# First layer's output, up and down projections: the second layer's order of products, wider products, and new places for weights and activations

## The chip, the cores and the metric

The kernel runs on one core of one Trainium2 chip. The metric is the device time of one execution in microseconds (us). Before the change it is 2280.66 us, the median of 3 runs (2280.07 to 2280.93).

## The reference

A decoder trunk of two layers over 272 positions (16 learned meta tokens and 256 inputs), width 2048, 16 heads of 128, MLP width 8192, all in float32. Cut to what matters here:

```python
a = rms_norm(h, norm_attn[0])
q, k, v, f = split(a @ fox_w_in[0])                # layer 0: forgetting attention
h = h + forgetting_attention(q, k, v, f) @ fox_w_o[0]
h = h + squared_relu(rms_norm(h, norm_mlp[0]) @ w_up[0]) @ w_down[0]
k, v = split(rms_norm(h, kv_norm) @ w_kv)          # layer 1: stick-breaking attention
q = rms_norm(h, norm_attn[1]) @ sb_w_q[0]
h = h + stick_breaking_attention(q, k, v) @ sb_w_o[0]
h = h + squared_relu(rms_norm(h, norm_mlp[1]) @ w_up[1]) @ w_down[1]
return rms_norm(h, final_norm)[:, 16:]
```

The first layer computes all 272 positions. The second layer's queries and all that follows need only the last 256, since the meta tokens are cut off at the end.

## The kernel before

Activations lie feature-major: 128 features on the partitions, 16 chunks of features, positions along the row. A product (`gemm_matmul`, line 190) is one 128x128 block of weights held in TensorE against one chunk of activations that streams past, 272 columns wide in the first layer (`t0` is 0) and in the K/V projection, 256 in the rest of the second layer (`t0` is 16). One word is 4 bytes.

**Two parts per number.** Each weight and each activation is split into a high and a low part, and three products are made: high by high, high weight by low activation, low weight by high activation. A weight block comes from HBM by a DMA on the SP queue (line 214) into `raw`; ScalarE writes the high part `whi` (line 225) and VectorE the low part `wlo` (line 226).

**A group** (`gemm_group`, line 230) makes 512 output features: 4 accumulators of PSUM (index `m`), 16 chunks of the inner dimension in 4 blocks `kb` of 4 chunks `kc`, 3 products each: 4 x 16 x 3 = 192 products. In blocks 0 and 3 the accumulators are taken one after the other, in blocks 1 and 2 all four over two chunks at a time (lines 248 to 251).

**The order of products** inside such a run differs (lines 255 to 258). In the first layer all products of one accumulator come first, and the three parts of a chunk follow one another. In the second layer the part is outermost: high by high over all chunks and accumulators of the run, then high by low, then low by high.

**The wider products** (lines 261 to 269). In the second layer, in the first group of each four (`u % 4 == 1`, where `u` numbers the groups), three products read 6 columns more, 262, from a pad of zeros that GpSimd (POOL) writes behind each chunk (line 135). The additional columns of the accumulator are not read.

**Places.** An x tile (`Split`, line 121) holds 16 chunks at a pitch of 640 words; the high part begins at `hi` and the low part at `lo`, 320 words on, from `ROWS`: (48, 368) in the first layer, (0, 320) in the second. A weight tile (line 217) has a pitch of 576 words per chunk, and its block begins at word `o1`: 0 in the first layer, 16 in the second. All x and weight buffers begin on a multiple of 64 words (256 bytes). There are two x buffers: one holds the input of a stage, the other its output.

**The stages around the change.** `out_proj` (line 612) makes the first layer's attention output, 4 groups, with input tile `o0`, and writes the tile `m0`. `mlp` (line 624) goes over the 8192 inner features in four quarters `f`: 4 groups of up projection from `m0`, whose evacuation squares and splits into the tile `u0_f` (lines 635 to 642), then 4 groups of down projection from `u0_f`, added to the residual. That makes 36 groups in the first layer's three projections. The three projections of the second layer use the same functions with `t0` = 16.

TensorE runs its instructions in program order. The order is fixed by the tile scheduler at build time, and `gemm_matmul` pins each product behind the one before it.

Of the kernel before, what the change touches and what calls it, by code (L numbers as in the profile page):

```python
# [24 lines left out]
N_FF = 4  # L25

ROWS = {0: (48, 368), M: (0, 320)}
XROW = 640

G_A0, G_M0, G_KV, G_A1, G_M1, G_FIN = range(6)  # L30
# [3 lines left out]
def yoco_kernel(ctx: ExitStack, tc: tile.TileContext, hT_in, gains, b_f, w_f, w_qkv0, w_o0, w_up, w_dn,  # L34
# [86 lines left out]
    class Split:  # L121


        def __init__(self, label, t0):
            n = T - t0
            self.t0 = t0
            rows = xs.tile([P, NC * XROW + 64], F32R, tag="x", name=f"x_{label}")
            hi, lo = ROWS[t0]
            rows = rows[:, hi:hi + NC * XROW].rearrange("p (c t) -> p c t", c=NC)
            d = lo - hi  # L130
            self.hi, self.lo = rows[:, :, :n], rows[:, :, d:d + n]
            if t0:

                self.wide = rows[:, :, :n + 6]
                nc.gpsimd.tensor_copy(rows[:, :, n:n + 6], pad[:, :6].unsqueeze(1).to_broadcast([P, NC, 6]))
# [65 lines left out]
    def weights(u, kb, wblk, o1, load_x=None):  # L201

        src_w = wblk[kb].rearrange("p (k c) -> p k c", k=4)
        piece = 1 if load_x is not None and kb < 2 else 2
        raws = [wraw.tile([P, 2, 512], F32, tag="raw", name=f"raw_{u}_{kb}_{hf}") for hf in range(2)]
        for k0 in range(0, 4, piece):
            if load_x is not None:
                load_x(range(4 * kb + k0, 4 * kb + k0 + piece))
            if load_x is not None and kb == k0 == 0:

                for c0 in (0, 256):
                    nc.scalar.dma_start(raws[0][:, 0, c0:c0 + 256], src_w[:, 0, c0:c0 + 256])
            else:
                nc.sync.dma_start(raws[k0 // 2][:, k0 % 2:k0 % 2 + piece], src_w[:, k0:k0 + piece])
        parts = []
        for hf in range(2):
            whi, wlo = (wspl.tile([P, 2, 576], F32R, tag=f"w{x}", name=f"w{x}_{u}_{kb}_{hf}") for x in ("hi", "lo"))
            whi, wlo = whi[:, :, o1:o1 + 512], wlo[:, :, o1:o1 + 512]
            boxes = [(o, piece, 0, 512) for o in range(0, 2, piece)]
            if load_x is not None and kb == hf == 0:  # L220
                boxes[:1] = [(0, 1, 0, 256), (0, 1, 256, 512)]
            for o, no, c0, c1 in boxes:
                src = raws[hf][:, o:o + no, c0:c1]
                hp, lp = whi[:, o:o + no, c0:c1], wlo[:, o:o + no, c0:c1]
                on_act = nc.scalar.activation(hp, src, AF.Copy)  # L225
                on_dve = nc.vector.tensor_tensor(out=lp, in0=src, in1=hp.bitcast(F32), op=ALU.subtract)  # L226
            parts.append((whi, wlo))
        return parts, on_act, on_dve

    def gemm_group(wblk, sp, t0, evac, before={}, after={}, load_x=None):  # L230

        uid[0] += 1
        u = uid[0]
        accs = [pacc.tile([P, 512], F32, tag="acc", name=f"acc_{u}_{m}") for m in range(4)]
        n = T - t0
        for kb in range(4):
            if kb in before:
                before[kb]()  # L240
            parts, on_act, on_dve = weights(u, kb, wblk, 16 if t0 else 0, load_x)
            if kb in after:
                with tc.issue_after(on_act.ins), tc.issue_after(on_dve.ins):
                    after[kb]()

            if load_x is not None and kb == 0:
                runs = [([kc], range(4)) for kc in range(4)]
            elif kb in (0, 3):
                runs = [(range(4), [m]) for m in range(4)]
            else:  # L250
                runs = [(range(2 * hf, 2 * hf + 2), range(4)) for hf in range(2)]
            pinned[0] = load_x is None
            for kcs, ms in runs:
                pairs = ((0, sp.hi), (0, sp.lo), (1, sp.hi))
                if t0:
                    products = [(kc, m, *pair) for pair in pairs for kc in kcs for m in ms]
                else:
                    products = [(kc, m, *pair) for m in ms for kc in kcs for pair in pairs]
                left = {m: 3 * len(kcs) for m in ms}

                wide = [(0, 0, 0), (1, 0, 1), (2, 1, 1)] if t0 and u % 4 == 1 else []
                if u == 90:

                    wide = [(0, 0, 0), (0, 0, 1), (0, 2, 1)]
                for kc, m, part, x in products:
                    first, left[m] = kb == kc == 0 and left[m] == 3 * len(kcs), left[m] - 1
                    nw = n
                    if m == (0 if u == 90 else 3) and x is sp.hi and (kb, kc, part) in wide:
                        x, nw = sp.wide, n + 6
                    gemm_matmul(accs[m][:, :nw], parts[kc // 2][part][:, kc % 2, m * P:(m + 1) * P], x[:, 4 * kb + kc],  # L270
                                start=first, stop=kb == kc == 3 and left[m] == 0)
                if kb == 3:
                    for m in ms:
                        evac(m, accs[m][:, :n])
# [39 lines left out]
    def load_x(chunks):  # L314
        c0, n = chunks[0], len(chunks)
        nc.sync.dma_start(hT[:, c0:c0 + n, :], hT_in[:, c0:c0 + n, :])
        if c0 == 0:
            nc.sync.dma_start(g_sb, gains)
        for c in chunks:
            split_chunk(xa, G_A0, c)  # L320
# [140 lines left out]
    ao = Split("o0", 0)  # L461
    for g in range(4):
# [11 lines left out]
        if g == 0:  # L474

            gemm_group(w_qkv0[0], xa, 0, lambda m, acc, qT=qT: nc.scalar.copy(qT[:, m, :], acc),
                       after={kb: (lambda kb=kb: first_norm(kb)) for kb in range(4)}, load_x=load_x)
# [12 lines left out]
        def decays(j):  # L490

            for i, (o, n) in enumerate(((0, 144), (144, T))):
# [5 lines left out]
                   after={j: (lambda j=j: decays(j)) for j in range(4)})  # L498
# [113 lines left out]
    def out_proj(w, ao, t0, gi, label):  # L612
        norm = Norm(label, t0)
        xm = Split(label, t0)
        for g in range(4):
            def evac(m, acc, g=g):
                c = 4 * g + m
                residual_add(c, acc, t0)
                split_chunk(xm, gi, c)
                norm.add(c)  # L620
            gemm_group(w[g], ao, t0, evac)
        return xm, norm

    def mlp(layer, xm, norm, t0, last_evac, last_group=None):
        box = {}

        def get_rstd():
            box["r"] = norm.finish()

        for f in range(N_FF):  # L630
            u = Split(f"u{layer}_{f}", t0)
            for g in range(4):
                def evac(m, acc, g=g):
                    c = 4 * g + m
                    r = tmp.tile([P, T], F32, tag="relu", name=f"relu_{layer}_{f}_{c}")
                    u2 = tmp.tile([P, T], F32, tag="u2", name=f"u2_{layer}_{f}_{c}")
                    nc.vector.scalar_tensor_tensor(out=r[:, t0:], in0=acc, scalar=0.0, in1=box["r"][:, t0:],
                                                   op0=ALU.max, op1=ALU.mult)
                    nc.scalar.activation(u2[:, t0:], r[:, t0:], AF.Square)
                    nc.scalar.activation(u.hi[:, c], u2[:, t0:], AF.Copy)  # L640
                    nc.vector.tensor_tensor(out=u.lo[:, c], in0=u2[:, t0:], in1=u.hi[:, c].bitcast(F32),
                                            op=ALU.subtract)
                gemm_group(w_up[layer, f, g], xm, t0, evac, {2: get_rstd} if f == g == 0 else {})
                if last_group is not None and f == N_FF - 1 and g == 0:
                    to_token_major()
            for g in range(4):
                def evac(m, acc, g=g):
                    residual_add(4 * g + m, acc, t0)
                    if f == N_FF - 1:
                        last_evac(4 * g + m)  # L650
                if last_group is not None and f == N_FF - 1 and g == 3:
                    last_group(w_dn[layer, f, g], u)
                else:
                    gemm_group(w_dn[layer, f, g], u, t0, evac)

    xm, norm_m = out_proj(w_o0, ao, 0, G_M0, "m0")


# [16 lines left out]
    for g in range(4):  # L675
# [4 lines left out]
        def split_c(kb, g=g):  # L680
            for c in ([4 * kb + g - 1] if g < 3 else [4 * kb + 2, 4 * kb + 3]):
# [3 lines left out]
                   after={kb: (lambda kb=kb: split_c(kb)) for kb in range(4)} if g else {})  # L685

    ao = Split("o1", M)
# [123 lines left out]
    xm, norm_m = out_proj(w_o1, ao, M, G_M1, "m1")  # L811
# [28 lines left out]
    def last_group(wblk, u):  # L840
        ob = xs.tile([P, NC * XROW + 64], F32, tag="x", name="ob")[:, :2 * D].rearrange("p (b d) -> p b d", b=2)

# [108 lines left out]
```

## Time and profile before

| what | value |
|---|---|
| timed runs, median of 3 | 2280.66 us |
| profiled execution, first to last instruction (span) | 2278.5 us |
| TensorE busy, share of the span | 2271.1 us, 100% |
| VectorE busy | 1333.5 us, 59% |
| ScalarE busy | 1065.1 us, 47% |
| GpSimd busy | 39.4 us, 2% |
| mean DMA rate | 187 GB/s |

The profile shows one execution. For the profiled execution the page gives the span; the time of a run is some 2 us longer than it. PE is TensorE's matmul, PEld its load of the stationary block. Matmuls overlap, so the duration of one (near 280 ns) is longer than the time from the start of one to the start of the next, and busy time says little here: the number to read is the time of a stretch divided by its count of products. The chain of work that ended last gives such stretches, as start, length, engine, tile, line and count.

### The profile page before, as it was taken

The numbers are of one execution on the slowest core, as the hardware profiler recorded it, in microseconds if no ns is written. First come the engines' busy times: TensorE is split into PE (matmuls) and PEld (weight loads), VectorE is DVE, ScalarE is ACT, GpSimd is POOL, SyncE is SP. The second block draws the span as 40 slices with busy tenths as digits, with TensorE's granted clock in tenths as the row PEclk, the third lists the DMA queues.
The fourth block names the chain that finished last, engine by engine and source line by source line (L and its number), as shares of the span: only waits on it lengthen the run. The fifth ranks groups of instructions, "written<-read, shape, count | busy, mean of one in ns | idle before, by whom it ended". The sixth has DMA issues, their size and how long they took to land.

```text
span 2278.5 us, 44956 instructions
## 1 busy us (share of the span) xinstructions
PE 2271.1 (100%) x18898; PEld 2262.8 (99%) x18898; DVE 1333.5 (59%) x1930; ACT 1065.1 (47%) x1471; POOL 39.4 (2%) x72
## 2 busy tenths in 40 slices
PE   9999999999999999999999999999999999999998
PEld 9999999999999999999999999999999999999998
DVE  7767566554455455455566666666555555555555
ACT  6444445443354344335445555555443544543554
POOL 1000000000000000000000000000000000000001
PEclk9999999999999999999999999999999999999999
DMA  7765665555555555555556555555656556566564
GB/s 238 228 198 188 222 184 176 181 172 180 182 176 185 167 185 179 174 185 169 186 183 193 168 174 169 167 185 190 202 187 201 192 189 201 184 200 195 186 201 141
DMA packets 146171, 425.19 MB, mean 187 GB/s; under 512 B 31648, under 2 KB 43824, under 8 KB 145968
## 3 DMA queue, kind: packets, MB, share of 16 engines
q1 hardware_dynamic: 113760, 406.29, 54.1%
q10 hardware_dynamic: 32208, 16.02, 2.6%
q8 instruction: 148, 2.42, 0.4%
q14 instruction: 55, 0.45, 0.1%
HBM read 413.85 MB, written 8.41 MB: 185 GB/s over the span
## 4 chain that ended last, share of the span: by engine, by line
PE 99%; DMA 0%; issue 0%; POOL 0%; SPq 0%; POOLq 0%; ACT 0%; DVE 0%
PE acc L192 97%; PE po L435 0%; PE ps L435 0%; PE pza L435 0%; DMA raw<-w_qkv 0%; PE pzb L735 0%; PE po L804 0%; PE ps L508 0%; PE po L603 0%; PE pf L354 0%; PE pta L757 0%; PE pta L756 0%; PE pv L394 0%; POOL ob L850 0%; PE ptb L709 0%
## 5 line engine op out<-in xcount | busy, mean ns | idle before, releaser
L226 DVE TENSOR_TENSOR wlo<-raw,whi 128x1024 fp32r<-128x1024 f32 (+1 forms) x773 | 928.5, 1216 | 715.6 <-ACT whi L225 706.6
L225 ACT ACTIVATE whi<-raw 128x1024 fp32r<-128x1024 f32 (+1 forms) x773 | 796.4, 1050 | 961.0 <-PE acc L192 913.4
L192 PE MATMUL acc<-x_m,whi 128*128 128x272 f32 (+1 forms) x4096 | 643.1, 282 | 0.0
L192 PE MATMUL acc<-x_u,whi 128*128 128x272 f32 (+1 forms) x3968 | 626.0, 282 | 0.0
L192 PEld LDWEIGHTS acc<-x_m,whi 128*128 128x128 f32 x4096 | 566.0, 188 | 0.1
L192 PEld LDWEIGHTS acc<-x_u,whi 128*128 128x128 f32 x3968 | 550.4, 188 | 0.0
L192 PE MATMUL acc<-x_m,wlo 128*128 128x272 f32 (+1 forms) x2048 | 441.4, 282 | 0.0
L192 PE MATMUL acc<-x_u,wlo 128*128 128x272 f32 (+1 forms) x1984 | 432.1, 282 | 0.0
L192 PE MATMUL acc<-x_a,whi 128*128 128x272 f32 (+1 forms) x2048 | 355.4, 286 | 0.2 <-ACT whi L225 0.2
L192 PEld LDWEIGHTS acc<-x_m,wlo 128*128 128x128 f32 x2048 | 323.5, 188 | 0.0
L192 PEld LDWEIGHTS acc<-x_u,wlo 128*128 128x128 f32 x1984 | 315.3, 188 | 0.0
L192 PEld LDWEIGHTS acc<-x_a,whi 128*128 128x128 f32 x2048 | 301.3, 189 | 1.7 <-ACT whi L225 1.1
L192 PE MATMUL acc<-x_a,wlo 128*128 128x272 f32 (+1 forms) x1024 | 253.8, 286 | 0.0
L192 PE MATMUL acc<-x_kv,whi 128*128 128x272 f32 x1024 | 191.7, 288 | 0.0
L192 PEld LDWEIGHTS acc<-x_a,wlo 128*128 128x128 f32 x1024 | 175.7, 188 | 0.7 <-DVE ssq_a L158 0.4
L192 PE MATMUL acc<-x_o,whi 128*128 128x272 f32 (+1 forms) x1024 | 163.1, 283 | 0.0
L192 PEld LDWEIGHTS acc<-x_kv,whi 128*128 128x128 f32 x1024 | 160.1, 189 | 0.1
L192 PE MATMUL acc<-x_kv,wlo 128*128 128x272 f32 x512 | 147.6, 288 | 0.0
L192 PEld LDWEIGHTS acc<-x_o,whi 128*128 128x128 f32 x1024 | 142.3, 188 | 0.0
L307 DVE TENSOR_TENSOR hT<-acc,hT 128x272 f32<-128x272 f32 (+1 forms) x156 | 67.3, 431 | 75.4 <-PE acc L192 75.2
L192 PE MATMUL acc<-x_o,wlo 128*128 128x272 f32 (+1 forms) x512 | 110.7, 282 | 0.0
L192 PEld LDWEIGHTS acc<-x_kv,wlo 128*128 128x128 f32 x512 | 96.6, 189 | 0.0
(255 smaller groups left out, 1065.5 us busy)
## 6 DMA issues: line engine op xcount, KB each, us to landing
raw<-w_up SPq DMA_DIRECT2D x256, 512.0 KB, 3.9
raw<-w_dn SPq DMA_DIRECT2D x256, 512.0 KB, 4.0
raw<-w_qkv SPq DMA_DIRECT2D x92, 512.0 KB, 4.3
raw<-w_o SPq DMA_DIRECT2D x64, 512.0 KB, 3.9
raw<-w_kv SPq DMA_DIRECT2D x64, 512.0 KB, 4.4
raw<-w_q SPq DMA_DIRECT2D x32, 512.0 KB, 4.7
p_dram<-raw_p ACTq DMA_DIRECT2D x32, 96.0 KB, 4.6
v_dram<-turned ACTq DMA_DIRECT2D x48, 64.0 KB, 3.8
```

The source lines that it names most:

```text
L192: ins = nc.tensor.matmul(*args, **kw).ins
L225: on_act = nc.scalar.activation(hp, src, AF.Copy)
L226: on_dve = nc.vector.tensor_tensor(out=lp, in0=src, in1=hp.bitcast(F32), op=ALU.subtract)
L307: nc.vector.tensor_tensor(out=hT[:, c, t0:], in0=acc, in1=hT[:, c, t0:], op=ALU.add)
```

## The change

The three projections of the first layer get the second layer's order of products (`series=True`) and its wider products (here 278 columns, still in the first group of each four), and the places of activations and weights are given per tile and per quarter:

| stage | hi, lo of the x tile | weight offset |
|---|---|---|
| output projection, before | 48, 368 | 0 |
| output projection, after | 0, 320 | 16 |
| up, quarters 0, 1, 2, 3, before | 48, 368 in all | 0 in all |
| up, quarters 0, 1, 2, 3, after | 0, 320 in all | 16, 0, 48, 32 |
| down, quarters 0, 1, 2, 3, before | 48, 368 in all | 0 in all |
| down, quarters 0, 1, 2, 3, after | 0, 320; 48, 368; 16, 336; 32, 352 | 16, 0, 16, 16 |

Every x tile but the first (`a0`) now gets its pad of zeros. The two x buffers change roles throughout the program. The number of products, the weights, the q/k/v, K/V and query projections, attention and the second layer's groups keep their code.

```diff
 ROWS = {0: (48, 368), M: (0, 320)}
+ROWS_OF = {"o0": (0, 320), "m0": (0, 320), "u0_0": (0, 320), "u0_2": (16, 336), "u0_3": (32, 352)}
...
-            hi, lo = ROWS[t0]
+            hi, lo = ROWS_OF.get(label, ROWS[t0])
...
-            if t0:
+            if label != "a0":
 
                 self.wide = rows[:, :, :n + 6]
                 nc.gpsimd.tensor_copy(rows[:, :, n:n + 6], pad[:, :6].unsqueeze(1).to_broadcast([P, NC, 6]))
...
-    def gemm_group(wblk, sp, t0, evac, before={}, after={}, load_x=None):
+    def gemm_group(wblk, sp, t0, evac, before={}, after={}, load_x=None, shift=None, series=None):
...
+        series = bool(t0) if series is None else series
...
-            parts, on_act, on_dve = weights(u, kb, wblk, 16 if t0 else 0, load_x)
+            parts, on_act, on_dve = weights(u, kb, wblk, shift if shift is not None else 16 if t0 else 0, load_x)
...
-                if t0:
+                if series:
                     products = [(kc, m, *pair) for pair in pairs for kc in kcs for m in ms]
...
-                wide = [(0, 0, 0), (1, 0, 1), (2, 1, 1)] if t0 and u % 4 == 1 else []
+                wide = [(0, 0, 0), (1, 0, 1), (2, 1, 1)] if series and u % 4 == 1 else []
...
-            gemm_group(w[g], ao, t0, evac)
+            gemm_group(w[g], ao, t0, evac, shift=16, series=True)
...
-                gemm_group(w_up[layer, f, g], xm, t0, evac, {2: get_rstd} if f == g == 0 else {})
+                gemm_group(w_up[layer, f, g], xm, t0, evac, {2: get_rstd} if f == g == 0 else {},
+                           shift=16 if t0 else (16, 0, 48, 32)[f], series=True)
...
-                    gemm_group(w_dn[layer, f, g], u, t0, evac)
+                    gemm_group(w_dn[layer, f, g], u, t0, evac, shift=16 if t0 else (16, 0, 16, 16)[f], series=True)
```

## The prediction

> **What bounds the kernel now.** I read the page's first part and chain first, then the waits of TensorE, then the chain in order of time, whose pieces give a time and a count of products together.
>
> ```profile
> span 2278.5 us, 44956 instructions
> ...
> PE 2271.1 (100%) x18898; PEld 2262.8 (99%) x18898; DVE 1333.5 (59%) x1930; ACT 1065.1 (47%) x1471; POOL 39.4 (2%) x72
> ...
> PEclk9999999999999999999999999999999999999999
> ...
> PE 99%; DMA 0%; issue 0%; POOL 0%; SPq 0%; POOLq 0%; ACT 0%; DVE 0%
> ```
>
> The page: TensorE is busy for the whole span, at full granted clock in every slice, and is 99% of the chain. Nothing else ends late. The waits of TensorE, all of them:
>
> ```profile
> PE idle L61 <- DVE mean_w L57: 1.1, 1, 1.1
> PE pr_fin L192 <- DVE fin L863: 0.8, 1, 0.8
> PE acc L192 <- ACT whi L225: 0.2, 1, 0.2
> ```
>
> So 2.1 us of 2278.5 are waits for data. The time is the number of products times the time from one product's start to the next; call that the step. The count does not change, so the question is what the change does to the step. The chain cut to stretches of one kind (start, us, what, count):
>
> ```profile
> 499.96 600.14 PE acc L192 x4866
> ...
> 609.97 80.05 PE acc L192 x649
> ...
> 704.94 80.17 PE acc L192 x650
> ...
> 1599.92 60.18 PE acc L192 x531
> ...
> 1493.92 2.83 PE acc L192 x24
> ...
> 1581.78 2.47 PE acc L192 x21
> ...
> 143.06 9.12 PE acc L192 x72
> ...
> 2246.88 7.33 PE acc L192 x32
> ```
>
> Row by row. Up and down of the first layer, 272 columns: 600.14/4866 = 123.33 ns. The same in an up stage (80.05/649 = 123.34) and a down stage (80.17/650 = 123.34), which read two different x buffers, so the buffer does not matter. Second layer, 256 columns, after the wider products: 60.18/531 = 113.33. Second layer before its first wider product: 2.83/24 = 117.9 and 2.47/21 = 117.6, say 117.8. A stretch of the q/k/v products of the first layer, 272 columns, the same code as its neighbours: 9.12/72 = 126.67. The last group, 512 columns: 7.33/32 = 229.1.
>
> What the reader is to see: for one width the step is not one number but one of a few, each held for dozens to thousands of products without scatter: 113.33 or 117.8 at 256 columns, 123.33 or 126.67 at 272. TensorE is in one of several states, and the question is in which the changed projections run. The mean duration of one product (last number before the last bar) tells the state too, and there are rows of it where a stretch is too short to count steps:
>
> ```profile
> L192 PE MATMUL acc<-x_m,whi 128*128 128x272 f32 x1594 | 295.1, 287 | 0.0
> ...
> L192 PE MATMUL acc<-x_a,whi 128*128 128x272 f32 x50 | 9.5, 290 | 0.0
> ...
> L435 PE MATMUL ps<-x_o,q x48: 286/289/384, 58.1 to 297.2; 128*128 128x272 f32 x48
> ...
> L435 PE MATMUL pza<-x_o,k x48: 277/280/287, 1289.3 to 1469.4; 128*128 128x256 f32 x48
> ...
> L192 PE MATMUL acc<-x_m,whi 128*128 128x256 f32 x337 | 43.4, 276 | 0.0
> ```
>
> 287 ns goes with a step of 123.33, 290 with 126.67; at 256 columns 276 goes with 113.33.
>
> **The change part by part.**
>
> Which products. Output projection 4 groups, up 16, down 16: 36 groups of 192 products, 6912 in all, each of 272 columns at 123.33 ns now, 852.5 us of the span. Everything else keeps its code; its x tiles swap buffers, which costs nothing by the rows of up and down above.
>
> Places. Let the distance be x offset less weight offset, in words modulo 64; chunk pitch 640, weight pitch 576, column block 128 and the 320 between hi and lo are multiples of 64, and all these buffers start on multiples of 256 bytes, so one distance holds for a whole group. Before, it is 48 - 0 = 48 in the first layer and 0 - 16 = 48 in the second. After: output 48; up by quarter 0-16, 0-0, 0-48, 0-32, that is 48, 0, 16, 32; down 0-16, 48-0, 16-16, 32-16, that is 48, 48, 0, 16. So 16 groups (3072 products) stay at 48 and 20 groups (3840 products) go elsewhere.
>
> The 3072 products at 48. Only the order and the wider products are new. Below they could fall to a state like the second layer's 113.33, above they could go to 126.67. By columns: the two states without lock, 117.8 at 256 and 229.1 at 512, differ by 111.3 ns over 256 columns, 0.435 ns per column; 113.33 + 16 x 0.435 = 120.3 ns would be the locked step at 272 columns, an estimate. The bounds are -3.0 and +3.3 ns, -9.3 and +10.2 us. I take 0: 123.33 holds through all 4866 products of the first row above without a push, and it lies nearer to a lock than the 117.8 + 7.0 = 124.7 that the columns give for a free run.
>
> The 3840 products elsewhere. No projection of the trace runs there. The nearest rows are attention's: its products at line 435 read the same x tiles against other stationary tiles, whose distances work out to 8 words (ps) and 24 words (pza). The 272-column one has a median of 289 where 48 has a mean of 287 and the slow stretch 290: two thirds of the way, 123.33 + 2.2 = 125.6 ns. The 256-column one has 280, against 276 locked. They are short runs between other work, so this is weak, but no row at a distance other than 48 shows a lock. Bounds: 120.3 if they lock (-11.6 us), 126.67 (+12.8 us); the free run of 124.7 gives +5.3. I take +2.2 ns: 3840 x 2.2 = +8.5 us.
>
> Order of products. The same 192 products, weights and sums. In blocks 0 and 3 the third product now needs chunk 2 of the weights where the seventh did, 4 steps or 0.5 us earlier. The waits above hold one wait of 0.2 us for a weight split in 2278 us, and the second layer runs this order at a shorter step without any, with as much split work per group (DVE and ACT have 59% and 47%). Cost 0; if that cover went, each late half would show as a wait of DVE or ACT at line 225 or 226.
>
> Wider products. The first group of each four from the output projection on has three of them: 9 x 3 = 27, each 6 columns more, 6 x 0.435 = 2.6 ns, 0.07 us, and in the state they leave there may be a settling step or two of some ns. I take 0.1 us.
>
> The pad copies that they read.
>
> ```profile
> L135 POOL CAST x_u<-pad x4: 267/267/268, 1570.5 to 2093.5; 128x96 fp32r<-128x96 f32 x4
> ...
> 1478.64 0.48 POOL L135 CAST x_m<-pad 128x96 fp32r<-128x96 f32 x1 [26.13 <-PE acc L192]
> 1479.48 1.15 POOL L446 COPY pk_vc<-vT 128x128 f32<-128x128 f32 x1 [0.36 <-DVE vT L472]
> ```
>
> Seven more copies on POOL of 0.27 to 0.48 us, each waiting for the last reader of its buffer. Behind that of x_m stand the packing copies of v, which TensorE's transposes need. The second layer has this very sequence: the copy behind it waited 0.36 us for DVE's v, not for the pad. Cost 0.
>
> Sum, on the profiled execution: 0 + 8.5 + 0.1 = +8.6 us on a span of 2278.5. The median of the timed runs is 2280.66, 2.2 us more than the span, for what lies around it; the sum goes on that: 2289.3 us.
>
> Two rules speak against any effect. The Trainium skill, SBUF — State Buffer, Who interferes with whom, says that TensorE reads moving and stationary operands through two independent ports and never waits on anyone; by that rule places change nothing and the time would be 2280.8. The Trainium skill, TensorE: Matmul & The Clock Gate, Back-to-back issue gap, gives columns/2.4 + 2.5 ns; by it 272 columns take 115.8 and the time would again not depend on places. The trace does not agree with the second (123.33 and 126.67 at one width and clock), and no run here shows the first.
>
> **The rivals.**
>
> (A) Lock everywhere. The wider product puts TensorE into a state that holds, as it does in the second layer; it decides at the first group of each four, up of quarter 0 for instance, and 768 products run at what it left. Price 6912 x -3.04 = -21.0 us: 2259.7, clearly faster. For it: the second layer goes from 117.8 to 113.33 at its wider products and keeps it through every stage. Against it: no 272-column row is below 123.33, though attention's products break and restart the q/k/v products again and again, and 123.33 may already be the 272-column form of that state.
>
> (B) Lock at distance 48 only, the others as now: 3072 x -3.04 = -9.3 us, 2271.4. With the others at +8.5, 2280.0, no change.
>
> (C) The change doesn't do what it says: neither order nor place moves the state, 2280.8.
>
> (D) The order loses 123.33 everywhere: 6912 x 3.33 = +23.0 us, 2303.8. For it: 126.67 is a stable state of the same width, held for 72 products and more in the trace, and a wider product may throw TensorE into it. Against it: in the first layer's long stages it never occurs.
>
> **How the numbers follow.** Forecast, 48 unchanged and the rest slower by 1.4 to 3.3 ns (2286 to 2294): 0.36. A 0.21, B with the others as now 0.14, B with the others slower 0.06, C 0.07, D 0.16. Against the 0.2% (4.6 us) that a measurement of this kernel can tell from no change: faster, A and B, 0.35; the same, 0.13 (C and the mixed B); slower, the forecast and D, 0.52. Cases of both signs hold much of this, so the range runs from A to a little over the forecast's upper bound, 2258 to 2297, and leaves out D; the forecast's own range is 2286 to 2294.
>
> **What would show it.** In the changed trace the chain in order of time, cut by half quarter (768 products each, now 94.7 us). Forecast: output, up 0, down 0 and down 1 at 123.3 ns; up 1, up 2, up 3, down 2 and down 3 between 124.7 and 126.7 (95.8 to 97.3 us). A shows as 92.4 us in each, C as 94.7, D as 97.3. Mean durations near 290 go with the slow state, near 284 with a lock. The forecast is wrong if a distance other than 48 runs below 123.3, if 48 leaves 123.3, or if TensorE gains waits at line 225, 226 or on POOL.

## The result, and the profile after

The changed kernel takes 2291.24 us (median of 4 runs, 2290.35 to 2291.56), the kernel before 2280.80 in the same sessions: a ratio of 1.0045, 95% interval 1.0030 to 1.0059. It is slower by 10.4 us, 0.45%. The profiled execution has a span of 2289.8 us, 11.3 more than before.

The page of the changed kernel, first parts:

```profile
span 2289.8 us, 44970 instructions
...
PE 2282.2 (100%) x18898; PEld 2273.8 (99%) x18898; DVE 1336.8 (58%) x1930; ACT 1065.5 (47%) x1471; POOL 42.4 (2%) x79
...
PEclk9999999999999999999999999999999999999999
```

TensorE is still busy throughout at full clock, with the same 18898 records. Its waits in the changed kernel:

```profile
PE idle L62 <- DVE mean_w L58: 1.1, 1, 1.1
PE pr_fin L193 <- DVE fin L866: 0.8, 1, 0.8
PE acc L193 <- ACT whi L226: 0.4, 1, 0.4
```

They come to 2.3 us against 2.1, so these waits do not make the 11.3 us (what the opening of the kernel adds stands below). The chain in order of time, one stretch from each stage (start, us, engine, tile, line, count of products); from the top: output; up and down of quarter 0; up and down of quarter 1; the same of quarters 2 and 3.

```profile
349.95 60.06 PE acc L193 x487
...
428.39 71.67 PE acc L193 x581
...
514.99 80.08 PE acc L193 x649
...
609.93 80.10 PE acc L193 x639
...
709.99 80.07 PE acc L193 x649
...
799.99 80.06 PE acc L193 x632
...
899.89 80.21 PE acc L193 x640
...
1000.00 80.05 PE acc L193 x632
...
1094.99 80.05 PE acc L193 x632
```

Divide: 123.33 ns in the output projection, 123.36 and 123.39 in up 0 and down 0, **125.35 in up 1** (distance 0), 123.37 in down 1, **126.68 in up 2** (16), **125.33 in down 2** (0), **126.66 in up 3** (32), **126.66 in down 3** (16). What the reader is to see: within the same 80 us the count falls from 649 to 639 or 632, and it does so exactly in the stages whose distance is not 48.

The whole difference, by the starts of the groups in both traces: 2 x 1.55 us at distance 0 and 3 x 2.55 at 16 and 32, 10.74 in all; the four stages at 48 together +0.23; three stretches of the v projections -0.25 each, -0.74; a delay among the q projections +0.15; and the opening of the kernel +0.94 (the second group starts at 33.58 us instead of 32.64). The last of these moves from run to run: in the experiments' profiles the second group starts between 32.23 and 33.31. It is probably most of why the profiled spans differ by 11.3 and the medians by 10.4.

### The profile page after: what moved, and what is told of

It is laid out like the page before. It is cut to its first block, busy times and chain, and to the rows that moved or that the text cites. A ratio compares the mean times of both kernels' runs of the same rounds, so it can differ in the third digit from the quotient of the medians.

```text
span 2289.8 us, 44970 instructions
## 1 busy us (share of the span) xinstructions
PE 2282.2 (100%) x18898; PEld 2273.8 (99%) x18898; DVE 1336.8 (58%) x1930; ACT 1065.5 (47%) x1471; POOL 42.4 (2%) x79
## 4 chain that ended last, share of the span: by engine, by line
PE 99%; DMA 1%; issue 0%; POOL 0%; DVE 0%; ACT 0%; POOLq 0%; SPq 0%; DVEq 0%; ACTq 0%
PE acc L193 96%; DMA raw<-w_qkv 1%; PE po L437 0%; PE ps L437 0%; PE pza L437 0%; PE pzb L738 0%; PE po L807 0%; PE ps L510 0%; PE po L605 0%; DMA hT<-hT_in 0%; PE pf L356 0%; PE pta L760 0%; PE pta L759 0%; PE pv L396 0%; POOL ob L853 0%
## 5 line engine op out<-in xcount | busy, mean ns | idle before, releaser
L193 PE MATMUL acc<-x_m,whi 128*128 128x256 f32 (+2 forms) x4096 | 552.3, 282 | 0.0
L193 PE MATMUL acc<-x_u,whi 128*128 128x272 f32 (+1 forms) x3968 | 533.5, 282 | 0.0
L193 PEld LDWEIGHTS acc<-x_m,whi 128*128 128x128 f32 x4096 | 515.7, 188 | 0.1
L193 PEld LDWEIGHTS acc<-x_u,whi 128*128 128x128 f32 x3968 | 498.4, 188 | 0.0
L193 PE MATMUL acc<-x_m,wlo 128*128 128x272 f32 (+1 forms) x2048 | 307.0, 282 | 0.0
L193 PE MATMUL acc<-x_u,wlo 128*128 128x272 f32 (+1 forms) x1984 | 297.1, 282 | 0.0
L193 PEld LDWEIGHTS acc<-x_m,wlo 128*128 128x128 f32 x2048 | 270.8, 188 | 0.0
L193 PEld LDWEIGHTS acc<-x_u,wlo 128*128 128x128 f32 x1984 | 261.8, 188 | 0.0
L639 DVE SCALAR_TENSOR_TENSOR relu<-acc,rstd_m 128x272 f32<-128x272 f32 (+1 forms) x128 | 55.5, 433 | 77.2 <-PE acc L193 76.7
L641 ACT ACTIVATE u<-relu 128x272 f32<-128x272 f32 (+1 forms) x128 | 53.9, 421 | 92.4 <-DVE relu L639 92.4
```

The costliest lines, as they stand in the source:

```text
L193: ins = nc.tensor.matmul(*args, **kw).ins
```

## The experiments

Theory **D**: the step of a 272-column product is set by the distance, x offset less weight offset modulo 64 words, and by nothing else in the change. Its rivals are named in each expectation. A wait or a delay that is put down to a place in the program is a difference between the starts of groups in that run's trace and in the trace of before. All steps below are time over count of a stretch of the chain.

**1. Order and wider products alone.**

```diff
-ROWS_OF = {"o0": (0, 320), "m0": (0, 320), "u0_0": (0, 320), "u0_2": (16, 336), "u0_3": (32, 352)}
+ROWS_OF = {}
...
-            gemm_group(w[g], ao, t0, evac, shift=16, series=True)
+            gemm_group(w[g], ao, t0, evac, series=True)
...
-                           shift=16 if t0 else (16, 0, 48, 32)[f], series=True)
+                           series=True)
```

(and the same for the down projection.)

> The changed kernel's order of products and wider products in the first layer's output, up and down projections, at the places of before (distance 48 in all 36 groups). Theory D (the step of a 272-column product is set by the distance, x offset less weight offset modulo 64 words): all 36 groups at 123.33 ns but for a few settling steps at the wider products, 94.72 us per stage of 768 products, 0.05 us more in each, the whole within 1 us of the kernel before. Rival O (the order or the wider products cost the time, the places do not): the up and down stages lengthen as in the changed kernel, by 1.5 to 2.6 us in at least five of eight, about 10 us in all.

The chain, a stretch of up 2 and one of down 3:

```profile
799.99 80.08 PE acc L193 x649
...
1084.89 80.21 PE acc L193 x650
```

The steps are 123.39 and 123.40 ns over these stretches, and 123.33 in the groups of these two stages that have no wider products. The run took 2281.74 us beside 2280.75 for the kernel before. Its profiled span is 1.5 us longer than that of before: 0.97 us of this is one wait near the start of the second head group, 0.15 the opening, and 0.35 the changed stages. The wait does not belong to the change: it is absent in the second experiment, and 1.10 us in the ninth, which leaves the first layer alone. Each up or down stage after the first lasts 94.76 us instead of 94.72; the 0.040 us are the price of three wider products. Order and wider products cost 0.35 us in all; rival O is out as the cause.

**2. Places alone.** `series=True` is taken out of the three calls, so that order and widths are those of before:

```diff
-                           shift=16 if t0 else (16, 0, 48, 32)[f], series=True)
+                           shift=16 if t0 else (16, 0, 48, 32)[f])
```

> The changed kernel's places with the order of before and no wider product in the first layer. Theory D: the steps of the changed kernel come back, 123.33 ns in up 0, down 0, down 1, 125.3 in up 1 and down 2 (distance 0), 126.67 in up 2, up 3 and down 3 (distances 16 and 32), about 10.7 us over the kernel before. Rival O: 123.33 ns in all stages and no loss.

The chain, up 1, down 1, up 2, down 2:

```profile
609.94 80.09 PE acc L193 x639
...
704.89 80.17 PE acc L193 x650
...
799.95 80.05 PE acc L193 x632
...
899.96 80.09 PE acc L193 x639
```

The steps are 125.34, 123.34, 126.66 and 125.34 ns: those of the changed kernel, without its order and its wider products. The run took 2290.82 us, 10.1 more than the kernel before. The places alone make the loss.

**3. Both moved together.**

```diff
+ROWS_OF = {"o0": (32, 352), "m0": (16, 336), "u0_0": (0, 320), "u0_1": (16, 336), "u0_2": (32, 352), "u0_3": (48, 368)}
...
+            gemm_group(w[g], ao, t0, evac, shift=16 if t0 else 48, series=True)
...
+                           shift=16 if t0 else 32, series=True)
...
+                    gemm_group(w_dn[layer, f, g], u, t0, evac, shift=16 if t0 else (16, 32, 48, 0)[f], series=True)
```

> The changed kernel with other places again, but weights and x moved together: x at words 32, 16, 0, 16, 32, 48 and weights at 48, 32, 16, 32, 48, 0, so that the distance is 48 in all 36 groups. Theory D: 123.33 ns in all stages, within 1 us of the kernel before. Rival P (the place of the weights or of x alone sets the step, for instance weights at words 0, 32 and 48 of the 64 being bad against x at 0): 125 ns or more in the stages whose weights stand at 32 or 48, up to 12 us in all.

Up 2 (weights at 32, x at 16) and down 2 (weights at 48, x at 32):

```profile
799.97 80.08 PE acc L193 x649
...
894.97 80.07 PE acc L193 x649
```

Both have 123.4 ns, and the run took 2280.73 us beside 2280.75. With weights at 32 and 48, x at 16 and 32, the loss is gone: rival P is out. Four pairs of places at distance 48 give one step here, and in the changed kernel the two pairs at distance 0 agree with each other, and so do the two at 16. For places that are multiples of 16 words it is the distance that counts in these stages, not either place.

**4. Finer distances.** Up: weights at 8, 24, 40, 56 against x at 0; down: x at 4, 60, 12, 20 against weights at 16.

```diff
+ROWS_OF = {"o0": (0, 320), "m0": (0, 320), "u0_0": (4, 324), "u0_1": (60, 380), "u0_2": (12, 332), "u0_3": (20, 340)}
...
+                           shift=16 if t0 else (8, 24, 40, 56)[f], series=True)
```

> The changed kernel with eight other distances in up and down of the first layer: up 56, 40, 24, 8, down 52, 44, 60, 4; output at 48. Theory D alone gives values between the neighbours measured at 48, 0, 16, 32 (123.33, 125.35, 126.67, 126.67 ns): 52 near 123.8, 56 near 124.3, 60 near 124.8, 4 near 125.7, 8 near 126.0, 24 at 126.67, 40 near 125, 44 near 124.2. Rival Q (only whole blocks of 16 words count): each distance runs like one of the four. Rival L (a lock exists for 272 columns at some finer distance): one stage at about 120.3 ns, 92.4 us for its 768 products.

Distances in order of time 56, 52, 40, 44, 24, 60, 8, 4:

```profile
444.97 65.11 PE acc L193 x514
...
544.91 65.11 PE acc L193 x514
...
639.98 65.12 PE acc L193 x528
...
734.99 65.12 PE acc L193 x528
...
829.92 65.17 PE acc L193 x520
...
925.00 65.12 PE acc L193 x521
...
1019.90 65.12 PE acc L193 x518
...
1114.95 65.08 PE acc L193 x523
```

The steps are 126.67, 126.67, 123.33, 123.33, 125.33, 124.99, 125.71 and 124.44 ns. This is neither a smooth curve (52 and 56 are as slow as 16) nor blocks of 16 words (40 and 32 differ), and no stage runs at 120.3: both refinements, theory D with values between its neighbours and rival Q, fell, and rival L has no support yet. The run took 2292.68 us.

**5. Eight further distances**, by the same kind of edit (up: weights 52, 44, 36, 28; down: x 54, 58, 62, 2), and then **6. eight distances again, made the other way** (up: weights 18, 22, 14, 26; down: x 44, 36, 52, 28).

> The changed kernel with eight further distances: up 12, 20, 28, 36, down 38, 42, 46, 50; output at 48. After the fine scan (40, 44, 48 at 123.33 ns, 52, 56, 16, 32 at 126.67, 0 and 24 near 125.4) the theory is that a band of distances from 40 to 48 holds 123.33 and nothing goes below: 42 and 46 at 123.33, 12 and 20 between 125.3 and 126.67, 28 and 50 at 126.67 or near it, 36 and 38 show the lower edge of the band. Rival L (a lock at a distance not yet tried): one stage at about 120.3 ns, 92.4 us for its 768 products.

Of experiment 5, distance 28 (up 2), 42 (down 1), 46 (down 2), 20 (up 1):

```profile
829.94 65.12 PE acc L193 x528
...
734.96 65.12 PE acc L193 x528
...
924.92 65.11 PE acc L193 x514
...
639.95 65.16 PE acc L193 x519
```

123.33, 123.33, 126.67 and 125.55 ns; 12 gave 125.71, and 36, 38 and 50 gave 126.67. The band from 40 to 48 is wrong, since 46 is slow and 28 is fast.

> The distances of the run with further distances, made the other way: up 46, 42, 50, 38 now by weights at words 18, 22, 14, 26 against x at 0 (there by x at 62, 58, 2, 54), down 28, 20, 36, 12 now by x at 44, 36, 52, 28 against weights at 16 (there by weights at 36, 44, 28, 52). Theory D, that the distance alone counts, also below 16 words: the same steps again, up 126.67, 123.33, 126.67, 126.67 ns, down 123.33, 125.6, 126.67, 125.7. Rival P (below 16 words the place of x or of the weights itself counts, or the history of the state does): at least two of the eight differ by more than 0.5 ns.

Of experiment 6, distance 46 (up 0), 42 (up 1), 50 (up 2), 36 (down 2) and 20 (down 1), made the other way:

```profile
444.99 65.12 PE acc L193 x528
...
634.97 65.08 PE acc L193 x523
...
824.99 65.12 PE acc L193 x528
...
919.97 65.08 PE acc L193 x523
...
729.93 65.13 PE acc L193 x521
```

123.33, 124.44, 123.33, 124.44 and 125.01 ns, where the same distances had 126.67, 123.33, 126.67, 126.67 and 125.55. Six of eight differ (12 too, 125.0 against 125.7); 28 and 38 came out the same. So theory D holds in these stages for places that are multiples of 16 words and falls below that. There what ran before counts. The trace of experiment 4 shows it within the first group of down 1 (distance 44), whose places do not change. Its wider products are the 37th, the 68th and the 120th; before the first, between the first and the last, and after the last:

```profile
706.58 4.32 PE acc L193 x35
...
711.65 9.37 PE acc L193 x74
...
721.92 8.14 PE acc L193 x66
```

That is 123.43, 126.62 and 123.33 ns at one pair of places: the step changes at one wider product and changes back at another (no run leaves them out here). So two makings of one distance can differ by what ran before them. Whether the places themselves count as well, these runs do not tell. In none of the 24 stages of the three runs is a step under 123.33; the two runs took 2295.27 and 2287.61 us.

**7. The second layer at the changed kernel's distances** (256 columns, on the kernel before).

```diff
-            hi, lo = ROWS[t0]
+            hi, lo = {"u1_1": (16, 336), "u1_2": (32, 352), "u1_3": (48, 368)}.get(label, ROWS[t0])
...
+                           shift=(16, 0, 48, 32)[f] if t0 else 0)
```

> The kernel before, with the second layer's up and down (256 columns, its order and wider products kept) at distance 48 in quarter 0, 0 in quarter 1, 16 in quarter 2 and 32 in quarter 3. Theory D: distance 48 keeps 113.33 ns (up 0, down 0); the others lose the lock and run at 117 ns or more, 2.8 us or more longer per stage of 768 products. Rival W (the wider products lock 256 columns at any distance): 113.33 ns in all.

Down 0 (distance 48), up 1 (0), up 2 (16), down 3 (32):

```profile
1684.96 55.08 PE acc L192 x486
...
1769.94 65.16 PE acc L192 x543
...
1959.99 55.12 PE acc L192 x468
...
2204.94 50.08 PE acc L192 x422
```

The steps are 113.33, 120.00, 117.78 and 118.67 ns, and the run took 2304.69 us. The other stages at these distances agree: 120.00 in down 1, 117.78 in down 2, 118.71 in up 3. The wider products do not bring 113.33 to other distances; rival W is out. Here distance 0 is the worst, at 272 columns it is the mildest of the three.

**8. Widths.** Zeros behind each chunk, and all products of the second layer's up and down widened into them; the added columns are read by nobody.

```diff
+                    if width is not None:
+                        nw = width + more
+                        x = (sp.rows_lo if x is sp.lo else sp.rows_hi)[:, :, :nw]
...
+                           width=(264, 272, 280, 260)[f] if t0 else None)
...
+                    gemm_group(w_dn[layer, f, g], u, t0, evac, width=(258, 268, 276, 288)[f] if t0 else None)
```

> The kernel before, with the second layer's up and down products widened by columns of zeros that nobody reads: up 264, 272, 280, 260 columns by quarter, down 258, 268, 276, 288; distance 48, order and pushes kept. Theory N (the 113.33 ns belongs to 256 columns, and 272 at distance 48 runs at 123.33 wherever it stands): up 1 at 123.33 ns, the others near 113.33 + 0.42 to 0.63 ns per column. Rival S (the lock belongs to the second layer's stage, and any width keeps its 6.7 ns over the columns' own time): up 1 at 120.3, the others at 113.33 + 0.43 ns per column: 114.2 at 258, 115.1 at 260, 116.8 at 264, 118.5 at 268, 122.0 at 276, 123.7 at 280, 127.1 at 288.

Widths 264, 258, 272, 268, 280 and 288:

```profile
1594.99 65.04 PE acc L197 x542
...
1689.98 60.05 PE acc L197 x497
...
1784.99 60.06 PE acc L197 x487
...
1879.89 65.23 PE acc L197 x515
...
1979.90 60.19 PE acc L197 x467
...
2239.94 70.12 PE acc L197 x526
```

The steps are 120.00, 120.83, 123.33, 126.66, 128.89 and 133.31 ns; 260 had 120.00 and 276 had 126.67. At 272 columns the second layer, with its order and wider products, runs at the first layer's 123.33: rival S is out. Two columns more than 256 cost 7.5 ns, and 268 is slower than 272. Theory N was right on 272 and wrong on the widths around it. The run took 2347.24 us.

**9. What holds the second layer's 113.33.** Quarter 1 in the first layer's order, quarter 2 without wider products, quarter 3 with both edits. The group behind the transposes (`u` = 90), which has three wider products of its own, loses them too.

```diff
-                if t0:
+                if t0 and not (73 <= u < 81 or u >= 89):
...
-                wide = [(0, 0, 0), (1, 0, 1), (2, 1, 1)] if t0 and u % 4 == 1 else []
+                wide = [(0, 0, 0), (1, 0, 1), (2, 1, 1)] if t0 and u % 4 == 1 and u < 81 else []
-                if u == 90:
+                if False:
```

> The kernel before with the second layer's quarters altered, all at distance 48: quarter 1 in the first layer's order of products, quarter 2 in its own order without wider products, quarter 3 with the first layer's order and without wider products. Theory D with a state that lasts: 113.33 ns in quarters 1 and 2, and in quarter 3 until the transposes of the token-major tail break the stream; whether 113.33 comes back after them without a wider product shows what the push is for. Rival H (the order holds the lock): 117.8 ns or more in up 1 and down 1 already, 3.4 us more per stage.

Up 1, up 2, and up 3 after the transposes:

```profile
1749.98 80.03 PE acc L192 x706
...
1924.89 80.13 PE acc L192 x707
...
2117.64 62.46 PE acc L192 x551
```

The steps are 113.36, 113.34 and 113.36 ns, and rival H is out. The run took 2281.88 us beside 2280.43; in its profile the wait near the start of the second head group is 1.10 us longer than in that of before. Neither the order nor the wider products are needed to keep the step, and after the transposes it came back by itself, within a few products. It is otherwise at three breaks earlier in the second layer, where the trace of before shows 117.8 for some 20 products (two of them are in the prediction's rows): there each such stretch ends at a wider product. Whether it would end without one was not tried.

**10. The gain inside the loss.** In the kernel before, the v projections of heads 4 to 15 each have a stretch at 126.67; in the changed kernel it is gone. One of them, in the kernel before and then the same products in the changed kernel:

```profile
220.22 10.64 PE acc L192 x84
```

```profile
221.07 10.37 PE acc L193 x84
```

The first has 126.67 ns, the second 123.45. The v projections read `a0` at words 48 and 368 and weights at word 0 in both kernels. So at distance 48, with places that are multiples of 16 words, 84 products can run at the slow step as well, by what ran before them; here the stretch follows attention's products and ends at the next break.

The kernel of this experiment moves only the tile `o0` to words 0 and 320 and the output projection's weights to 16, on the kernel before.

> The kernel before with one place moved: the tile o0 at words 0 and 320 and the output projection's weights at 16, so that the projection's own distance stays 48, while attention's products of the q/k/v stage read o0 at another distance from their stationary tiles. Theory D: the output projection stays at 123.33 ns; the stretches of 70 and more products at 126.67 ns in the v projections of heads 4 to 15 are gone as in the changed kernel, 0.24 to 0.27 us each, 0.8 us in all: about 2279.9 us, a ratio of 0.9997, hardly outside the interval. Rival B (those stretches went because the two x buffers changed roles): no change.

The groups behind the three v projections start earlier by 0.27, 0.27 and 0.24 us. In this kernel the x buffers keep their roles; in the first experiment they changed roles while `o0` kept its place, and nothing was gained. So the place of `o0` is the cause and rival B is out. The time is 2279.70 us beside 2280.43, a ratio of 0.9998 with an interval of 0.9989 to 1.0007: the 0.8 us are seen in the trace and cannot be told from nothing in the time.

## Why the prediction was right

The forecast was 2289.3 us, and 2291.24 were measured. The case that came was the likeliest one of the list, distance 48 unchanged and the rest slower, and the time lies in that case's own range of 2286 to 2294. The whole range, 2258 to 2297, held faster times too and says little. The cause was right; that the total came within 2 us is partly luck, since the places cost 2.2 us more than the forecast had and a gain of 0.74 us that it did not have took some of this back. Step by step:

- **The bound.** Right: the count of records did not change, waits stayed near 2 us, and the loss is counts of products per 80 us.
- **The 3072 products at 48, taken at 0.** Right: 123.33 ns in all four stages, but for the wider products, +0.23 us together.
- **The 3840 elsewhere, taken at +2.2 ns.** Right in kind, too small: 1536 products at distance 0 cost 2.0 ns and 2304 at 16 and 32 cost 3.3, a mean of 2.8 and 10.7 us instead of 8.5. The row that set the price was attention's product at a distance of 8 words (median 289). At 8 words the fourth experiment measured 125.71, 0.1 ns over the 125.6 read off that row. That closeness is luck: the row is a median in whole nanoseconds between 287 and 290, and below 16 words the distance alone does not set the step. What failed was to carry the row to three other distances.
- **The remark that no row away from 48 shows the better step** was true of that trace and is not a rule: 28, 40 and 44 reach 123.33, and 42, 46 and 50 did in one of their two makings.
- **Order, pads.** Cost 0, confirmed by the first experiment and by the list of waits.
- **Wider products, taken at 0.1 us.** Too small: 0.35 us by the first experiment, 0.04 for three of them, where 6 columns each would make 0.008 by the prediction's rate. The rest is settling behind them.
- **The lock and its price.** The step of 120.3 ns for a lock at 272 columns came from a rate of 0.435 ns per column. The eighth experiment has no such rate, and 272 columns run at 123.33 in the second layer too. That the wider products put the second layer into 113.33 was read from stretches that end at them; the ninth experiment shows that they are not needed to keep it.
- **Not foreseen:** the -0.74 us in the v projections. The new place of `o0` is read by attention's products, and they leave TensorE in another step. The prediction priced the moved tile in its own projection only.
- **Rivals.** A and B: no 272-column stage went below 123.33, in either layer, at any place tried. C forecast no change, and 10.4 us are well clear of the noise. D: the first experiment has 123.33 with the new order everywhere. A change to the slow step at a wider product is seen at distance 44 (experiment 4); at 48 none is.

The Trainium skill, SBUF — State Buffer, Who interferes with whom, has TensorE reading its two operands through independent ports and waiting on nobody. By it the third experiment and the changed kernel would run alike; they differ by 10 us through the places of TensorE's own two operands. What happens inside is not shown by any run here.

The prediction also sets a formula, columns/2.4 + 2.5 ns, against the trace. The Trainium skill, TensorE: Matmul & The Clock Gate, Back-to-back issue gap, gives it for one product by itself and says of a stream of loads and products that both set the spacing. So 123.33 ns in this stream does not contradict it.

## What to carry to other kernels

When TensorE is busy for the whole span, divide stretches of the chain by their counts: the step shows losses that busy shares hide, and stages with different settings in one run make a scan. Try each setting behind different predecessors, since what ran before can count. Where weights and activations lie relative to each other within 256 bytes was worth 3.3 ns in 123 at 272 columns and 6.7 in 113 at 256; keep their distance when you move them, or scan it, and expect neither a smooth curve nor a setting that carries over to another width.

## What the runs showed of the hardware that was not expected

- Every lasting step, as a mean over a stretch, is close to a simple multiple of 6.667 ns: 113.33 is 17, 117.78 is 17 2/3, 118.67 is 17 4/5, 120.00 is 18, 120.83 is 18 1/8, 123.33 is 18 1/2, 124.44 is 18 2/3, 125.00 is 18 3/4, 125.33 is 18 4/5, 125.55 is 18 5/6, 125.71 is 18 6/7, 126.67 is 19, 128.89 is 19 1/3, 133.33 is 20. Single starts are not spaced so: at 123.33 they lie 121 to 125 ns apart. TensorE may fall into step with something of that period; this is read off the numbers alone, fractions with denominators up to 8 lie close together, and no run shows what it would be.
- One pair of places can hold two steps, by what ran before: 126.62 and 123.33 ns at distance 44 within one group of experiment 4, and 126.67 and 123.45 at distance 48 in the v projections.
- Width does not act column by column: 258 columns cost more than 264, and 272 cost less than the next widths tried on either side, 268 and 276.
